# State-space layer: six PSUM banks in the ring, state outputs of two tiles in four array quarters, a reordered end of the gated unit

## The chip, the cores and the metric

The kernel runs on one core of one Trainium2 chip. The metric is the device time of one execution in microseconds (us). A core has TensorE (PE: matmuls, and transposes as matmuls against an identity), VectorE (DVE), ScalarE (ACT), GpSimd (POOL) and SyncE (SP, which here issues most of the DMAs), and sixteen DMA engines that carry what the queues hold. PSUM, into which PE writes, has eight banks of 2 KB in each of 128 partitions.

## The reference, cut to what matters

Two layers on 512 tokens of width 1024. Layer 0 mixes tokens by a diagonal complex state space (64 groups of 16 channels, 64 states each), followed by a gelu and a gated linear unit; layer 1 is attention. A dense feed-forward net follows layer 0, eight routed experts follow layer 1. The change lies in the mixer of layer 0:

```python
bu_re = jnp.einsum('bsgc,gpc->sbgp', ug, bb_re)
bu_im = jnp.einsum('bsgc,gpc->sbgp', ug, bb_im)
...
_, _, s_re, s_im = lax.associative_scan(_s5_combine, (a_re, a_im, bu_re, bu_im), axis=0)
y = (jnp.einsum('sbgp,gcp->bsgc', s_re, c_re.astype(f32))
     - jnp.einsum('sbgp,gcp->bsgc', s_im, c_im.astype(f32)))
y = y.reshape(bsz, seq, D_MODEL) + d_skip.astype(f32) * uf
act = jax.nn.gelu(y).astype(u.dtype)
val, gate = jnp.split(act @ w_glu, 2, axis=-1)
return val * jax.nn.sigmoid(gate)
...
x = _layer_norm(ALPHA * x + mix, ln_g[layer, 0], ln_b[layer, 0])
```

## The kernel before, in words

**The scan in blocks.** The 512 tokens are 64 blocks (j) of 8 steps (t). Inside a block the mixer is a matrix (Toeplitz blocks `s_T`, made from `s_K` by `s5_k`); between blocks a state `s_S` is carried by a scan on DVE over numbers that are turned to a rotating frame before it and back after it (`turn`, L1899: three DVE passes, L1905, L1906 and L1909, through the scratch tile `s5_ctv`). Complex products of coefficients go through `cmul` (L1798), in steps of at most 512 elements of each part, with the same scratch tile when DVE does them. All of it is done for two halves of the groups: half 0 feeds output pairs `dp` 0 and 1, half 1 pairs 2 and 3.

**The outputs.** `s5_y(dp)` (L2003) makes two output tiles i of [64 blocks, in two halves of 64 partitions for the parity of the group; 4 groups pairs q x 128 columns], each in one PSUM bank. For each q there are two matmuls of `s_T` (L2017: 128 rows, 64 columns of the array) and four of the state (L2021: 64 rows and 64 columns, real and imaginary part), in the order T T S S S S for each of the four q. ACT takes the gelu (L2023), and the result is also written to DRAM (`YD`, used only by a fallback path). `s5_act(dp)` (from L2031) transposes it (L2044), 16 transposes to a pair, and ACT and DVE split it in a high and a low half-precision part `xt` (L2047, L2048).

**The gated unit.** `w_glu` has 1024 x 2048 numbers. It is taken in four quarters of columns (256 of value, 256 of gate), and each quarter in two chunks of 1 MB, 8 chunks in all. A chunk is loaded by eight DMAs of [128 partitions, 256 columns] (`Stream.load`, L85), converted to two half-precision parts by ACT and DVE (`Stream.convert`, L102 and L103), and used by 48 matmuls with `mm3` (L275 to L277: three products for each pair of parts). All these DMAs are issued by SyncE in the program's order, as are X (L2127), the gain and bias of the norm (`gb`, L197) and the feed-forward weights behind them; chunk 0 comes early in the scan, chunk 1 behind the transfers that spread `s_K` (L2000). The unit's rows are ordered as the transposes leave them: in the weight's row index (k g r c) a tile has the eight values of g and the sixteen of c on its partitions.

**Where the two meet.** `glu_quarter` runs the first two quarters in four steps kp and calls `before(kp)` at each, for the first quarter this function of `run` (L2051):

```python
            def before(kp):
                if kp == 2:
                    self.s5_y(2)
                    self.s5_y(3)
                    self.s5_act(2)
                    self.s5_act(3)
                if kp == 3:
                    st.convert(3)
```

**The end of the unit.** `glu_last` (L307) does the last quarter token tile by token tile, in an order written out by hand in `GLU_ORDER` (L54): M is a tile's 24 matmuls, E its sigmoid and sum, s a step of its layer norm, T the transposes of the normalised tile (L261, L264, L265) for the feed-forward net, c a conversion of that net's weights, a and b the net's first blocks on the first and the second 256 tokens. PSUM banks are handed out by `bank()` from a ring of `nps`: 5 during the scan, 8 from the gated unit on; the other banks of the scan belong to the pool `pt` (the scratch tile and the coefficients `s5_pwp`).

Of the kernel before, what the change touches and what calls it, by code (L numbers as in the profile page):

```python
# [15 lines left out]
D = 1024  # L16
# [4 lines left out]
L = 8  # L21
# [29 lines left out]

GLU_FAST = (2, 3)
MLA_ORDER = "O0 R0 s0 s0 O1 R1 s1 s0 s1 O2 R2 s2 s1 s2 T0 O3 R3 s3 s2 s3 p0 T1 s3 g0 a0 T2 a1 A0 T3 a2 A1 r0 a3 q0 A2 r1 v0 q1 v1 t0 A3 r2 v2 t1 q2 r3 k0 v3 t2 q3 t3"
GLU_ORDER = "M0 c2 E0 s0 M1 M2 E1 s1 s0 s1 s0 s1 T0 E2 s2 s2 T1 M3 E3 s2 s3 s3 s3 a0 T2 T3 a1 b0 c4 c3 b1"  # L54
RSQRT = 519526879.0


# [66 lines left out]
class Kernel:  # L124
# [154 lines left out]

    def glu_chunks(self):  # L280

        w = self.A["s5_w_glu"][0].rearrange("(k g r c) (v n) -> k r g c v n", k=4, r=2, c=GC, v=2)
        return [[(w[kp, r, :, :, v, q * 256:(q + 1) * 256], o + v * 256, o + (v + 1) * 256, None)
                 for kp in (k2, k2 + 1) for r in range(2) for v in range(2) for o in ((kp - k2) * 1024 + r * 512,)]
                for q in range(4) for k2 in (0, 2)]

    def glu_mms(self, acc, tt, kp, w):

# [1082 lines left out]
    def general(self, flag):  # L1371
# [6 lines left out]
        with tc.If(reg > 0):  # L1378
# [77 lines left out]
                    V.tensor_copy(xt[:, 2 * dp:2 * dp + 2].rearrange("p r (j t) -> p r t j", t=L)[:, :, t0:t0 + 4],  # L1456
                                  b.rearrange("p (t r j) -> p r t j", t=4, r=2))
            nc.sync.dma_start(X, A["x"][0].rearrange("(t p) d -> p t d", p=128))
            wg = A["s5_w_glu"][0].rearrange("(k g r c) (v n) -> k r g c v n", k=4, r=2, c=GC, v=2)
            for c in (slice(0, 512), slice(512, 1024)):  # L1460
                b = [[bank() for _ in range(TT)] for _ in range(2)]
                for k in range(KD):
                    for v in range(2):
                        w = weights(wg[k // 2, k % 2, :, :, v, c])
                        for tt in range(TT):
                            mm(b[v][tt], xt[:, k, tok(tt)], w, start=k == 0, stop=k == KD - 1)
                for tt in range(TT):
# [198 lines left out]
    def s5_params(self):  # L1666
# [73 lines left out]
        for i in range(3):  # L1740
# [4 lines left out]
                V.tensor_sub(P[:, i, 0], t[:, 0], t[:, 1])  # L1745
                V.scalar_tensor_tensor(P[:, i, 2], re, 2.0, im, op0=OP.mult, op1=OP.mult)
            V.tensor_scalar(P[:, i, 1::2], P[:, i, 2, None, :].to_broadcast([128, 2, 32]), -1.0, None, op0=OP.mult)
        self.pwp = self.pt.tile([128, 3, 4, 32], F, name="s5_pwp")
        nc.scalar.activation(self.pwp, P, AF.Copy)
        self.bb = self.r3.tile([128, 2, 32, GC], F, name="s5_bb")  # L1750
        self.cmul(V, self.bb, self.b, f, 0, 32)
# [46 lines left out]
    def cmul(self, eng, dst, x, cf, g0, g1, conj=False, one=None):  # L1798


        n = x.shape[3]
        step = min(g1 - g0, 512 // n)
        cr = cf[:, 0, None, :, None]
        ci = cf[:, 2:4] if conj else cf[:, 1:3]
        nm = "s5_ctv" if eng is self.nc.vector else "s5_ctp"
        for g in range(g0, g1, step):
            s = slice(g, g + step)
            sh = [128, 2, step, n]
            if eng is self.nc.vector:
                t = self.pt.tile([128, 2, 512], F, name=nm, tag=nm, bufs=1)[:, :, :step * n]  # L1810
            else:
                t = self.r3.tile([128, 2, 512], F, name=nm, tag=nm, bufs=1)[:, :, :step * n]
            t = t.rearrange("p a (g n) -> p a g n", n=n)
            xs = x[:, :, s]
            eng.tensor_mul(t, self.swap(xs), ci[:, :, s, None].to_broadcast(sh))
            if n >= 64 and eng is self.nc.vector:
                for i in range(step):
                    eng.scalar_tensor_tensor(dst[:, :, g + i], x[:, :, g + i], one[:, 0, g + i:g + i + 1], t[:, :, i],
                                             op0=OP.mult, op1=OP.add)
                continue  # L1820
            eng.tensor_mul(dst[:, :, s], xs, cr[:, :, s].to_broadcast(sh))
            eng.tensor_add(dst[:, :, s], dst[:, :, s], t)
# [76 lines left out]
    def turn(self, dst, x, E, back):  # L1899
        V = self.nc.vector  # L1900
        sh = list(x.shape)
        t = self.pt.tile([128, 2, 512], F, name="s5_ctv", tag="s5_ctv", bufs=1).rearrange(
            "p a (i n) -> p (a i n)", n=4 * NJ)[:, :8 * NJ]
        t = t.rearrange("p (a g n) -> p a g n", a=2, g=4)[:, :, :, :sh[3]]
        V.tensor_mul(t, self.swap(x), E[:, 1, None].to_broadcast(sh))  # L1905
        V.tensor_mul(dst, x, E[:, 0, None].to_broadcast(sh))  # L1906
        for part in range(2):
            op = V.tensor_add if back == (part == 0) else V.tensor_sub
            op(dst[:, part], dst[:, part], t[:, part])  # L1909
# [92 lines left out]

    def s5_y(self, dp):  # L2003

        nc = self.nc
        mm = nc.tensor.matmul
        y = self.r1.tile([128, L, 2, 4, GC], F, name="s5_y", tag="s5_y", bufs=2)
        T = self.T[dp // 2]
        halves = [slice(par * 64, par * 64 + 64) for par in range(2)]
        for i in range(2):  # L2010
            dt = 2 * dp + i
            p = self.bank()
            for q in range(4):
                pr = dt * 4 + q
                c = slice(q * 128, (q + 1) * 128)
                for par, rows in enumerate(halves):
                    mm(p[rows, c], self.U[:, 2 * pr + par], T[:, (q % 2 * 2 + par) * 8 + q // 2 * 4 + dt % 4], start=True, stop=False,  # L2017
                       tile_position=(0, par * 64))
                for part in range(2):
                    for par, rows in enumerate(halves):  # L2020
                        mm(p[rows, c], self.S[rows, part, pr, 0:NJ], self.O[rows, part, pr], start=False,  # L2021
                           stop=part == 1, tile_position=(par * 64, par * 64))
            nc.scalar.activation(y[:, :, i].rearrange("j t q c -> j q t c"),  # L2023
                                 p.rearrange("j (q t c) -> j q t c", q=4, t=L), AF.Gelu_apprx_tanh)
        self.ydt[dp] = y
        nc.gpsimd.dma_start(self.YD[dp * 128:(dp + 1) * 128], y.rearrange("p t i q c -> p (t i q c)"))
# [24 lines left out]
    def run(self):  # L2051
# [6 lines left out]

        self.YD = dram.tile([SEQ, D], F, name="YD")
        if phases != "moe":  # L2060
            self.ps = self.pool("psS", None, space=bass.MemoryType.PSUM)
            self.nps = 5
            self.pt = self.pool("psT", None, space=bass.MemoryType.PSUM)
        else:
            self.ps = self.pool("psA", None, space=bass.MemoryType.PSUM)
        self.wp = self.pool("w", "right")
# [1 line left out]
        if phases != "moe":  # L2068
# [47 lines left out]
            self.bz = None  # L2116
            self.s5_scan(1, E[1])
            E = self.dec = None
            self.pt.release()
            self.ps.release()  # L2120
            self.nps = 8
            self.ps = self.pool("psA", None, space=bass.MemoryType.PSUM)
            st.load(2)
# [8 lines left out]
            def before(kp):  # L2132
                if kp == 2:
                    self.s5_y(2)
                    self.s5_y(3)
                    self.s5_act(2)
                    self.s5_act(3)
                if kp == 3:
                    st.convert(3)

            self.glu_quarter(0, st, before)
# [102 lines left out]
```

## Time and profile before

| | us |
|---|---|
| median of three runs | 1849.55 (1846.19 to 1849.65) |
| the profiled execution | 1850.73 |
| its span in the trace | 1849.0 |
| PE busy | 1721.1, 93% of the span |
| DVE busy | 1399.1, 76% |
| ACT busy | 1001.2, 54% |
| last scan matmul to first of the gated unit | 117.45 to 125.17 |
| first matmul of the last quarter (M0) | 207.73 |
| first matmul of the feed-forward net (a0) | 237.67 |

The profiled execution takes 1.73 us more than its span, which lies around it. PE is the engine that is busiest and also the one that the end of the program waits for most; the stretch that the change touches ends at a0, after 13% of the span. Times below are from the start of the span. A timeline row gives the start, the length, the line and the tiles of one or more like instructions, and in brackets how long the engine stood idle before them and what released it. The length of a matmul in a row contains its way through the array; matmuls follow each other faster than that, so a rate is read from the starts of successive rows.

### The profile page before, as it was taken

How to read it: one execution, taken by the hardware profiler on the slowest of the kernel's cores; microseconds unless marked ns; L12 is line 12 of the kernel's file. 1: busy time of each engine (PE TensorE's matmuls, PEld its weight loads, DVE VectorE, ACT ScalarE, POOL GpSimd, SP SyncE). 2: the span in 40 equal slices, each digit the busy share in tenths (PEclk: the TensorE clock that was granted, in tenths of full speed). 3: DMA queues.
4: the chain of work that ended last, by engine and by line, in shares of the span. 5: the costliest groups of instructions: out<-in, count | busy, mean ns of one | idle time of the engine just before them, and what ended most of it. 6: DMA issues, size and time to landing. Idle time of an engine off the chain costs nothing.

```text
span 1849.0 us, 45063 instructions
## 1 busy us (share of the span) xinstructions
PE 1721.1 (93%) x19531; PEld 1360.6 (74%) x19531; DVE 1399.1 (76%) x2040; ACT 1001.2 (54%) x1100; POOL 223.4 (12%) x232
## 2 busy tenths in 40 slices
PE   5689899999999898789999999999999999999984
PEld 4455464444446564589999999999999899999863
DVE  9863653333246784589999898999999799999987
ACT  4223432323142673277676666767667676766771
POOL 6910100000000101100000121210000100000035
PEclk9889999999999999789999999999999999999997
DMA  4236423332352000299999999999999999999991
GB/s 81 52 110 212 118 69 109 96 103 80 136 151 88 1 24 24 105 380 376 359 328 347 343 340 331 325 365 350 362 351 351 286 377 378 362 368 365 353 365 60
DMA packets 359393, 433.79 MB, mean 235 GB/s; under 512 B 30520, under 2 KB 321424, under 8 KB 359184
## 3 DMA queue, kind: packets, MB, share of 16 engines
q1 hardware_dynamic: 346832, 417.55, 67.0%
q0 software_dynamic: 4064, 12.72, 2.4%
q8 instruction: 155, 2.54, 0.6%
q10 hardware_dynamic: 8288, 0.54, 0.4%
q14 instruction: 54, 0.44, 0.1%
HBM read 416.81 MB, written 11.34 MB: 232 GB/s over the span
## 4 chain that ended last, share of the span: by engine, by line
PE 77%; DVE 12%; ACT 3%; DMA 3%; issue 3%; POOL 1%; POOLq 0%; DVEq 0%; ACTq 0%; SPq 0%
PE gu L275 10%; PE gu L277 10%; PE gu L276 10%; PE ps L276 7%; PE ps L277 7%; PE ps L275 7%; PE y L275 5%; PE y L277 5%; PE y L276 5%; DVE wi L1110 2%; PE gu L1058 2%; DMA mraw<-in_moe_w_in_dram 2%; PE glu L277 1%; PE glu L275 1%; PE glu L276 1%
## 5 line engine op out<-in xcount | busy, mean ns | idle before, releaser
L277 PE MATMUL gu<-xe,wi 128*128 128x132 f16 (+7 forms) x3584 | 660.3, 225 | 17.8 <-DVE wi L1110 17.7
L275 PE MATMUL gu<-xe,wi 128*128 128x132 f16 (+7 forms) x3584 | 660.5, 225 | 6.1 <-ACT yr L1195 4.1
L276 PE MATMUL gu<-xe,wi 128*128 128x132 f16 (+7 forms) x3584 | 660.3, 225 | 0.0
L1110 DVE SCALAR_TENSOR_TENSOR wi<-mraw,wi 128x2048 f16<-128x2048 f32 x224 | 512.0, 2286 | 9.0 <-ACT wi L1104 9.0
L1104 ACT ACTIVATE wi<-mraw 128x2048 f16<-128x2048 f32 x224 | 420.5, 1904 | 26.5 <-DMA mraw<-in_moe_w_in_dram 25.6
L277 PEld LDWEIGHTS <-wi 128*128 128x128 f16 x3584 | 352.7, 98 | 19.4 <-DVE wi L1110 19.4
L276 PEld LDWEIGHTS <-wi 128*128 128x128 f16 x3584 | 354.1, 99 | 9.2 <-issue 4.5
L275 PEld LDWEIGHTS <-wi 128*128 128x128 f16 x3584 | 353.2, 99 | 5.8 <-ACT wi L1104 2.1
L1110 DVE SCALAR_TENSOR_TENSOR wol<-mraw,woh 128x2048 f16<-128x2048 f32 x112 | 255.8, 2284 | 0.3 <-ACT woh L1104 0.3
L1104 ACT ACTIVATE woh<-mraw 128x2048 f16<-128x2048 f32 x112 | 213.3, 1904 | 7.8 <-DMA mraw<-in_moe_w_out_dram 7.8
L277 PE MATMUL y<-hh,wol 128*128 128x132 f16 (+4 forms) x1120 | 215.9, 227 | 0.0
L275 PE MATMUL y<-hh,woh 128*128 128x132 f16 (+4 forms) x1120 | 215.9, 227 | 0.0
L276 PE MATMUL y<-hl,woh 128*128 128x132 f16 (+4 forms) x1120 | 215.9, 227 | 0.0
L1127 ACT ACTIVATE hs<-gu 128x168 f32<-128x168 f32 (+5 forms) x224 | 63.8, 285 | 273.5 <-PE gu L277 273.1
L103 DVE SCALAR_TENSOR_TENSOR wf<-raw,wf 128x2048 f16<-128x2048 f32 x34 | 77.9, 2292 | 95.7 <-ACT wf L102 81.1
L1162 POOL DMA_INDIRECT XD<-yr,at x12 | 26.4, 2204 | 810.0 <-ACT yr L1195 444.3
L275 PE MATMUL ps<-xt,wf 128*128 128x512 f16 x320 | 121.3, 379 | 0.0
L276 PE MATMUL ps<-xt,wf 128*128 128x512 f16 x320 | 121.3, 379 | 0.0
L277 PE MATMUL ps<-xt,wf 128*128 128x512 f16 x320 | 121.3, 379 | 0.0
L1128 DVE SCALAR_TENSOR_TENSOR hf<-gu,hs 128x168 f32<-128x168 f32 (+5 forms) x224 | 66.7, 298 | 60.0 <-ACT hs L1127 59.3
L275 PEld LDWEIGHTS <-woh 128*128 128x128 f16 x1120 | 109.6, 98 | 0.0
L276 PEld LDWEIGHTS <-woh 128*128 128x128 f16 x1120 | 109.6, 98 | 0.1
(460 smaller groups left out, 2792.2 us busy)
## 6 DMA issues: line engine op xcount, KB each, us to landing
mraw<-in_moe_w_in_dram SPq DMA_DIRECT2D x224, 1024.0 KB
mraw<-in_moe_w_out_dram SPq DMA_DIRECT2D x112, 1024.0 KB
raw<-in_ffn_w_in_dram SPq DMA_DIRECT2D x44, 512.0 KB
raw<-in_ffn_w_out_dram SPq DMA_DIRECT2D x11, 1024.0 KB
raw<-in_s_w_glu_dram SPq DMA_DIRECT2D x64, 128.0 KB
raw<-in_mla_o_w_dram SPq DMA_DIRECT2D x4, 1024.0 KB
XD<-X SPq DMA_DIRECT2D x5, 512.0 KB
xj<-in_x_dram SPq DMA_DIRECT2D x4, 512.0 KB
```

What stands on the lines that cost most here:

```text
L103: nc.vector.scalar_tensor_tensor(lo[:, c], raw[:, c], scale[j], hi[:, c], op0=OP.mult, op1=OP.subtract)
L275: mm(out, lh, rh, start=first, stop=False, **kw)
L276: mm(out, lh, rl, start=False, stop=False, **kw)
L277: mm(out, ll, rh, start=False, stop=last, **kw)
L1058: nc.tensor.matmul(p[:, (k - k0) * cap:(k - k0 + 1) * cap], x[:, tt, k * 128:(k + 1) * 128], sel[:, tt, :cap], start=tt == 0, stop=tt == T ...
L1104: nc.scalar.activation(hi, raw, AF.Copy, scale=WS)
L1110: self.nc.vector.scalar_tensor_tensor(lo, raw, WS, hi, op0=OP.mult, op1=OP.subtract)
L1127: nc.scalar.activation(sg, p[:, :cap], AF.Silu, scale=1.0 / (WS * XS))
L1128: nc.vector.scalar_tensor_tensor(h, p[:, cap:2 * cap], HS / (WS * XS), sg, op0=OP.mult, op1=OP.mult)
L1162: self.nc.gpsimd.indirect_dma_start(out=self.XD, out_offset=bass.IndirectOffsetOnAxis(ap=self.at[:n, j:j + 1], axis=0), in_=yr[:n], in_off ...
```

## The change

Five edits: (1) the ring of the scan has six banks instead of five, for which the scratch tile is halved and `cmul` on DVE takes steps of 256 elements instead of 512; (2) `s5_y` is split in `s5_yt`, the T matmuls of both tiles, and `s5_ys`, the state matmuls of both tiles side by side, where the second tile's two parities land in swapped halves of the partitions, so that four consecutive state matmuls use the four quarters of the array; (3) the swap permutes the rows that the gated unit's weights must have, and each of its weight DMAs becomes two of 64 partitions; (4) the T matmuls of y(3) go ahead of the transposes of y(2), and `s5_act(3)` moves to kp 3; (5) in `GLU_ORDER` M3 goes ahead of T0, and a1 ahead of T2. The diff, cut (a fallback path that isn't run here gets the same two DMAs):

```diff
-GLU_ORDER = "M0 c2 E0 s0 M1 M2 E1 s1 s0 s1 s0 s1 T0 E2 s2 s2 T1 M3 E3 s2 s3 s3 s3 a0 T2 T3 a1 b0 c4 c3 b1"
+GLU_ORDER = "M0 c2 E0 s0 M1 M2 E1 s1 s0 s1 s0 s1 M3 T0 E2 s2 s2 T1 E3 s2 s3 s3 s3 a0 a1 T2 T3 b0 c4 c3 b1"
...
-        w = self.A["s5_w_glu"][0].rearrange("(k g r c) (v n) -> k r g c v n", k=4, r=2, c=GC, v=2)
-        return [[(w[kp, r, :, :, v, q * 256:(q + 1) * 256], o + v * 256, o + (v + 1) * 256, None)
-                 for kp in (k2, k2 + 1) for r in range(2) for v in range(2) for o in ((kp - k2) * 1024 + r * 512,)]
+        return [[(src, o + v * 256, o + (v + 1) * 256, view)
+                 for kp in (k2, k2 + 1) for r in range(2) for v in range(2) for o in ((kp - k2) * 1024 + r * 512,)
+                 for src, view in self.glu_rows(kp, r, v * D + q * 256, 256)]
                 for q in range(4) for k2 in (0, 2)]
+
+    def glu_rows(self, kp, r, c, n):
+        w = self.A["s5_w_glu"][0]
+        row = 2 * D
+        return [(bass.AP(tensor=w.tensor, offset=w.offset + (kp * 16 + i * 8 + (r ^ i)) * GC * row + c,
+                         ap=[[2 * GC * row, 4], [row, GC], [1, n]]), lambda d, i=i: d[i * 64:i * 64 + 64]) for i in range(2)]
...
-        step = min(g1 - g0, 512 // n)
+        step = min(g1 - g0, (256 if eng is self.nc.vector else 512) // n)
...
-                t = self.pt.tile([128, 2, 512], F, name=nm, tag=nm, bufs=1)[:, :, :step * n]
+                t = self.pt.tile([128, 2, 256], F, name=nm, tag=nm, bufs=1)[:, :, :step * n]
...
+    def s5_yt(self, dp):
...
         for i in range(2):
             dt = 2 * dp + i
             p = self.bank()
             for q in range(4):
+                for par in range(2):
+                    o = (par ^ i) * 64
+                    mm(p[o:o + 64, q * 128:(q + 1) * 128], self.U[:, 2 * (dt * 4 + q) + par],
+                       T[:, (q % 2 * 2 + par) * 8 + q // 2 * 4 + dt % 4], start=q == 0, stop=False,
+                       tile_position=(0, o), skip_group_check=True)
...
+        for q in range(4):
+            for part in range(2):
+                for i, p in enumerate(ps):
+                    pr = (2 * dp + i) * 4 + q
+                    for par in range(2):
+                        rows = slice(par * 64, par * 64 + 64)
+                        o = (par ^ i) * 64
+                        mm(p[o:o + 64, q * 128:(q + 1) * 128], self.S[rows, part, pr, 0:NJ], self.O[rows, part, pr],
+                           start=False, stop=part == 1 and q == 3, tile_position=(par * 64, o), skip_group_check=True)
...
-            self.nps = 5
-            self.pt = self.pool("psT", None, space=bass.MemoryType.PSUM)
+            self.pp, self.pt, self.ps = (self.pool("ps" + n, None, space=bass.MemoryType.PSUM) for n in "ptS")
+            self.nps = 6
...
                 if kp == 2:
                     self.s5_y(2)
-                    self.s5_y(3)
+                    late = self.s5_yt(3)
                     self.s5_act(2)
+                    self.s5_ys(3, late)
+                if kp == 3:
                     self.s5_act(3)
-                if kp == 3:
                     st.convert(3)
```

How the instructions stand. First SyncE's queue from the second half's `s_K` transfers to the feed-forward weights, before (`raw` is a chunk of weights as loaded):

```order
L2000 DMA s_T<-s_K 32x8x32 x3
L85 DMA raw<-in_s_w_glu_dram 128x1x256 x8
L2127 DMA X<-in_x_dram 128x4x1024
L85 DMA raw<-in_s_w_glu_dram 128x1x256 x16
L197 DMA gb<-in_ln_g_dram 128x1024
L197 DMA gb<-in_ln_b_dram 128x1024
L85 DMA raw<-in_s_w_glu_dram 128x1x256 x32
L85 DMA raw<-in_ffn_w_in_dram 128x8x128 x44
```

and now:

```order
L2007 DMA s_T<-s_K 32x8x32 x3
L85 DMA raw<-in_s_w_glu_dram 64x1x256 x16
L2152 DMA X<-in_x_dram 128x4x1024
L85 DMA raw<-in_s_w_glu_dram 64x1x256 x32
L197 DMA gb<-in_ln_g_dram 128x1024
L197 DMA gb<-in_ln_b_dram 128x1024
L85 DMA raw<-in_s_w_glu_dram 64x1x256 x64
L85 DMA raw<-in_ffn_w_in_dram 128x8x128 x44
```

The order is the same; each weight DMA stands there as two of half the partitions.

Second, PE inside the first quarter, where y(2) and y(3) stand between the unit's steps kp 1 and kp 2. Before, the two rows of the start repeat sixteen times, and the transposes of both pairs follow together (`s_U` are the inputs, `s_O` the output coefficients, `s_y` the pair's result):

```order
L2017 MATMUL ps<-s_T,s_U 64x128 x2
L2021 MATMUL ps<-s_O,s_S 64x128 x4
L2017 MATMUL ps<-s_T,s_U 64x128 x2
L2021 MATMUL ps<-s_O,s_S 64x128 x4
...
L2044 MATMUL ps<-ident,s_y 128x128 x16
```

and now:

```order
L277 MATMUL glu<-wf,xt 128x512
L2026 MATMUL ps<-s_T,s_U 64x128 x16
L2044 MATMUL ps<-s_O,s_S 64x128 x32
L2026 MATMUL ps<-s_T,s_U 64x128 x16
L2068 MATMUL ps<-ident,s_y 128x128 x8
L2044 MATMUL ps<-s_O,s_S 64x128 x32
L275 LDWEIGHTS xt
L275 MATMUL glu<-wf,xt 128x512
```

PE changes between T and state matmuls four times instead of 32; the transposes of y(2) stand between T and state of y(3), and those of y(3) come after kp 2.

Third, PE at the end of the unit, where the transposes of the normalised tiles 0 and 1 (L261) stand. Before, M3 (matmuls into `glu`) follows them:

```order
L277 LDWEIGHTS xt
L277 MATMUL glu<-wp,xt 128x512
L261 MATMUL ps<-ident,X 128x128 x16
L275 LDWEIGHTS xt
L275 MATMUL glu<-wp,xt 128x512
```

and now it is ahead of them, and the feed-forward net's a0 (matmuls into `ps`) follows:

```order
L277 LDWEIGHTS xt
L277 MATMUL glu<-wp,xt 128x512
L261 MATMUL ps<-ident,X 128x128 x16
L275 LDWEIGHTS wp
L275 MATMUL ps<-xt,wp 128x256
```

The 24 matmuls of M3 have gone past T0 and T1.

## Rows read from the trace of the kernel before

**Rows 1.** Section 4 of the page, the chain that ended last, by engine
```profile
PE 77%; DVE 12%; ACT 3%; DMA 3%; issue 3%; POOL 1%; POOLq 0%; DVEq 0%; ACTq 0%; SPq 0%
```

**Rows 2.** Windows: stretch, length, busy of each engine, clock, DMA share, GB/s
```profile
157.00:211.00 54.00, 54.00 (x252) 24.49 (x251) 25.21 (x44) 19.02 (x21) 0.00 (x0) 1.00 0.70 201
162.00:178.00 16.00, 16.00 (x76) 7.28 (x75) 5.72 (x13) 4.48 (x6) 0.00 (x0) 1.00 0.55 184
186.00:204.00 18.00, 18.00 (x85) 8.16 (x84) 8.41 (x9) 6.13 (x5) 0.00 (x0) 1.00 1.02 271
1000.00:1400.00 400.00, 398.14 (x5716) 375.38 (x5715) 367.38 (x473) 272.44 (x247) 45.35 (x33) 1.00 1.02 347
```

**Rows 3.** Timeline of PE: start, length, line, operation, [idle before <- releaser]
```profile
106.75 0.44 PE L1988 MATMUL ps<-s_O,s_bz 128*64 128x128 f32 x4
...
125.17 0.58 PE L275 MATMUL glu<-wf,xt 128*128 128x512 f16 x1 [7.73 <-DVE s_S L1909]
...
130.67 0.43 PE L276 MATMUL glu<-wf,xt 128*128 128x512 f16 x1
```

**Rows 4.** Timeline of SyncE's queue (SPq), 118 to 180 us, and 161.57 to 178.45
```profile
126.54 5.20 SPq L85 DMA_DIRECT2D raw<-in_s_w_glu_dram  x8
...
132.35 17.49 SPq L85 DMA_DIRECT2D raw<-in_s_w_glu_dram  x16
...
161.58 16.86 SPq L85 DMA_DIRECT2D raw<-in_s_w_glu_dram  x24
```

**Rows 5.** DMA issues in 118 to 215 us: transfer, queue, count, KB each, us
```profile
YD<-s_y POOLq DMA_DIRECT2D x2, 512.0 KB, 6.6
```

**Rows 6.** Timeline of ACT, 137 to 219 us
```profile
137.66 1.91 ACT L102 ACTIVATE wf<-raw 128x2048 f16<-128x2048 f32 x1 [19.56 <-DMA raw<-in_s_w_glu_dram]
...
208.21 3.70 ACT L102 ACTIVATE wp<-raw 128x2048 f16<-128x2048 f32 x2
...
218.29 0.38 ACT L347 ACTIVATE glu_s<-glu 128x256 f32<-128x256 f32 x1 [1.19 <-PE glu L277]
```

**Rows 7.** Timeline of DVE, 55 to 237 us
```profile
55.05 0.69 DVE L1905 TENSOR_TENSOR s_ctv<-ps,s_E 128x504 f32<-128x504 f32 x1 [4.18 <-PE ps L1893]
...
79.49 0.74 DVE L1909 TENSOR_TENSOR s_S<-s_S,s_ctv 128x252 f32<-128x252 f32 x2
...
87.49 1.23 DVE L1815 TENSOR_TENSOR s_ctv<-s_O,s_pwp 128x1024 f32<-128x1024 f32 x1
...
98.20 0.69 DVE L1905 TENSOR_TENSOR s_ctv<-ps,s_E 128x504 f32<-128x504 f32 x1
...
210.15 4.49 DVE L103 SCALAR_TENSOR_TENSOR wp<-raw,wp 128x2048 f16<-128x2048 f32 x2 [0.90 <-ACT wp L102]
...
235.23 1.28 DVE L265 TENSOR_TENSOR xt<-ps,xt 128x512 f16<-128x512 f32 x2
```

**Rows 8.** Timeline of PE at the end of the gated unit
```profile
210.32 0.38 PE L275 MATMUL glu<-wp,xt 128*128 128x512 f16 x1
...
227.80 1.94 PE L261 MATMUL ps<-ident,X 128*128 128x128 f32 x8 [4.36 <-DVE X L249]
...
237.67 0.27 PE L275 MATMUL ps<-xt,wp 128*128 128x256 f16 x1
...
245.35 1.09 PE L261 MATMUL ps<-ident,X 128*128 128x128 f32 x8 [1.40 <-DVE X L219]
```

**Rows 9.** Timeline of PE in y(0), y(1), and in the block products after it
```profile
83.37 0.44 PE L2017 MATMUL ps<-s_T,s_U 128*64 128x128 f32 x4
83.74 0.65 PE L2021 MATMUL ps<-s_O,s_S 64*64 64x128 f32 x8
84.32 0.44 PE L2017 MATMUL ps<-s_T,s_U 128*64 128x128 f32 x4
...
98.61 0.69 PE L1893 MATMUL ps<-s_U,s_at 128*64 128x64 f32 x16
99.23 0.66 PE L1876 MATMUL ps<-ident,s_A 128*128 128x128 f32 x4
```

More of the change, by code (lines that the diff above doesn't have):

```diff
@@ L1458, in general @@
             nc.sync.dma_start(X, A["x"][0].rearrange("(t p) d -> p t d", p=128))
-            wg = A["s5_w_glu"][0].rearrange("(k g r c) (v n) -> k r g c v n", k=4, r=2, c=GC, v=2)
             for c in (slice(0, 512), slice(512, 1024)):
@@ L1463, in general @@
                     for v in range(2):
-                        w = weights(wg[k // 2, k % 2, :, :, v, c])
+                        w = p.tile([128, 512], F, name="gw0", tag="gw0", bufs=2)
+                        for src, view in self.glu_rows(k // 2, k % 2, v * D + c.start, 512):
+                            nc.sync.dma_start(view(w), src)
                         for tt in range(TT):
@@ L1747, in s5_params @@
             V.tensor_scalar(P[:, i, 1::2], P[:, i, 2, None, :].to_broadcast([128, 2, 32]), -1.0, None, op0=OP.mult)
-        self.pwp = self.pt.tile([128, 3, 4, 32], F, name="s5_pwp")
+        self.pwp = self.pp.tile([128, 3, 4, 32], F, name="s5_pwp")
         nc.scalar.activation(self.pwp, P, AF.Copy)
@@ L1901, in turn @@
         sh = list(x.shape)
-        t = self.pt.tile([128, 2, 512], F, name="s5_ctv", tag="s5_ctv", bufs=1).rearrange(
-            "p a (i n) -> p (a i n)", n=4 * NJ)[:, :8 * NJ]
+        t = self.pt.tile([128, 2, 256], F, name="s5_ctv", tag="s5_ctv", bufs=1).rearrange("p a n -> p (a n)")
         t = t.rearrange("p (a g n) -> p a g n", a=2, g=4)[:, :, :, :sh[3]]
@@ L2003, in s5_y @@
     def s5_y(self, dp):
-        nc = self.nc
-        mm = nc.tensor.matmul
-        y = self.r1.tile([128, L, 2, 4, GC], F, name="s5_y", tag="s5_y", bufs=2)
+        self.s5_ys(dp, self.s5_yt(dp))
+    def s5_yt(self, dp):
+        mm = self.nc.tensor.matmul
         T = self.T[dp // 2]
-        halves = [slice(par * 64, par * 64 + 64) for par in range(2)]
+        ps = []
         for i in range(2):
@@ L2013, in s5_y, with s5_ys @@
             for q in range(4):
[L2014 to L2022, printed above, removed]
+                for par in range(2):
[3 more added lines that the diff above has]
+                       tile_position=(0, o), skip_group_check=True)
+            ps.append(p)
+        return ps
+    def s5_ys(self, dp, ps):
+        nc = self.nc
+        mm = nc.tensor.matmul
+        y = self.r1.tile([128, L, 2, 4, GC], F, name="s5_y", tag="s5_y", bufs=2)
+        for q in range(4):
[7 more added lines that the diff above has]
+                           start=False, stop=part == 1 and q == 3, tile_position=(par * 64, o), skip_group_check=True)
+        for i, p in enumerate(ps):
             nc.scalar.activation(y[:, :, i].rearrange("j t q c -> j q t c"),
@@ L2060, in run @@
         if phases != "moe":
-            self.ps = self.pool("psS", None, space=bass.MemoryType.PSUM)
-            self.nps = 5
-            self.pt = self.pool("psT", None, space=bass.MemoryType.PSUM)
+            self.pp, self.pt, self.ps = (self.pool("ps" + n, None, space=bass.MemoryType.PSUM) for n in "ptS")
+            self.nps = 6
         else:
@@ L2118, in run @@
             E = self.dec = None
-            self.pt.release()
-            self.ps.release()
+            self.pwp = None
+            for p in (self.ps, self.pt, self.pp):
+                p.release()
             self.nps = 8
```

## The prediction

> **What bounds the kernel now.** The page first: TensorE (PE) makes 77% of the chain that ended last [rows 1]. The change touches only the state-space layer and the gated unit behind it, the first 250 us, so next I read, stage by stage, how busy PE is there, then the order of PE, DVE and ACT and what each wait ended on. From 157 to 211 us PE has 54.00 busy of 54.00 [rows 2]: in the unit every microsecond of PE is paid for. Ahead of the unit it isn't: PE stands 7.73 us for the last unrotation on DVE [rows 3]. Last I looked at what feeds the unit, since its weights arrive while it runs. In 162 to 178 us nothing but these weights moves: the DMA engines are busy 0.55 of the time at 184 GB/s. When the feed-forward weights move (sources of 128 rows side by side), the same queue has a share of 1.02 at 271 GB/s, and with the experts' weights 347 GB/s [rows 2]. SyncE issued 24 of the unit's transfers, 128 KB each, in 16.86 us, 0.7025 us each, against 0.65 (8 in 5.20) when nothing was ahead of them; and 16 issues right behind X's 2 MB took 17.49 us, 1.09 each [rows 4]. So SyncE was held back by transfers with half the engines idle: those of the unit use about half of the sixteen. That is the reading on which my forecast hangs.
>
> **The change, part by part.** The sum is made against the profiled execution, 1850.73 us, 1.18 above the median of the three runs; 1.2 comes off at the end.
>
> *1. Weight transfers.* One transfer of 128 rows, in 8 blocks of 16, becomes two of 64 rows, in 4 blocks of 16: 112 instead of 56 for chunks 1 to 7. A source of 8 blocks has half the engines busy, one of 128 has all [rows 2]: as if a block went to an engine as a whole. Then 4 blocks have a quarter of them, a half-size transfer lasts as long as a whole one did, 0.7025 us, and a chunk of 1 MB takes 16 x 0.7025 = 11.24 us instead of 5.62. PE eats a chunk in 10.4 us (48 matmuls of 0.2157), so weights turn from cover into bound. No row shows a source of 4 blocks; the bounds are 5.62 us a chunk (half the time each) and 11.24, and I take the upper, because the trace has the busy engines at their limit, not the bytes.
> The Trainium skill (DMA: Bandwidth & Descriptors, "Why a DMA increments its semaphore by 16 and not by 1") says that a transfer is spread over the largest number up to 16 that divides the slowest dimension of both sides, on the lowest-numbered engines: 8 before, 4 after. The trace's 0.55 agrees for 8; no run here shows 4 yet.
>
> *2. Start of the stream.* It waits for the second half's Toeplitz blocks (s5_k), whose transfers leave SyncE's queue at 126.54; s5_k starts on PE at 106.75, behind the gelu transposes [rows 3, 4]. After, those come earlier and s5_k waits instead for the third turn's read of a bank: turns start at 98.20 today [rows 7], 0.74 later by step 7, and run back to back at 2.13, the read ends 1.36 into its turn: 98.94 + 4.26 + 1.36 = 104.5. So 2.2 us earlier, 124.3 (bounds 124.3 and 126.5).
>
> *3. When chunk 7 lands.* 7 x 11.24 = 78.7. The same engines carry X (128x4x1024, 2.1 MB), ln_g and ln_b (128x1024 each, 1.05 MB together) and two writes of YD (1.05 MB) [rows 5]: 4.2 MB at 347 GB/s = 12.1. From the last issue to the landing: 5.9 us at most (chunk 1: 131.74 to ACT's start at 137.66, with X moving too), 0 at least; 2 taken, since SyncE is held back until near the end [rows 4, 6]. 124.3 + 78.7 + 12.1 + 2 = 217.1. ACT converts the chunk in 1.85 and DVE follows with 2.25 (half of 3.70 and of 4.49) [rows 6, 7]: 221.2. Before, PE took up that chunk at 210.32 [rows 8]: **+10.9**.
>
> *4. Clock.* PE is then idle for 7 to 8 us ahead of it (chunk 6 carries it to about 213). After the 7.73 us ahead of 125.17, 13 matmuls took 5.5 us instead of 2.8 [rows 3]: **+2.7**. M0 ends at 221.2 + 5.1 and M1 at 231.5.
>
> *5. The end of the unit.* Before, 9.5 us passed from the sigmoid of M1 (218.29) to T0 (227.80) [rows 6, 8]: tile 0 is normalised at 241.0. M2 and M3 now both run first, 2 x 5.18, to 241.9; M3 fills the 4.36 us in which PE stood before T0. T0 to the last eviction of T1 took 227.80 to 236.51, 8.7 us [rows 7, 8]; a0 needs only its first half, 0.6 sooner: 250.0. Before, a0 began at 237.67: **+12.4** so far, which is steps 3 and 4 less what the new order gives. PE stands about 5 us ahead of a0, for which the clock can cost 0 to 2.7; I take **+1.3**. With a1 ahead of T2 and T3 their wait of 1.40 us goes [rows 8], but b0 now stands right behind T3 and waits about as long for its eviction: 0. On ACT the conversion of two feed-forward chunks (c2) stands ahead of E0; they are queued behind chunk 7 and land about 6 us after it (2.1 MB at 347), converted near 228, still ahead of M1's end: 0, and 3 to 5 if they land late.
>
> *6. The state outputs.* y(2) and y(3) take 16 x 0.95 = 15.3 us on PE: 0.37 for four T records and 0.58 for eight S records, of which 0.16 a step is the change of array mode, as 16 records elsewhere take 0.62 [rows 9]. After: T 16 x 0.105 = 1.7, S between 1.7 (four quarters at once) and 3.4 (two), 2.5 taken, two changes of mode: 4.5 for a pair, 9.0 for both. Of the 6.3 saved, the gelu of y(2) and the transposes of y(3) show about 2 as waits: -4.3 (-2 to -5). It only brings PE sooner to chunks that aren't there: **0** in the sum. For y(0) and y(1) the saving lies under DVE: the S products wait for both unrotations of their pair (79.49 + 0.74 for the first) and DVE works on, alone, to 98.0 [rows 7].
>
> *7. cmul cut to 256 elements.* A 128x1024 step of 1.23 becomes two of 0.69 [rows 7]. Ahead of 98.0 one block of three such steps gains 0.44 and two of one such step 0.15 each: 0.74. In the preparation before 55.05 some 1.9 us are added, under DVE's 4.18 us of idle time there [rows 7]. The unit's start moves by 0 to +1, which PE then waits for anyway: 0.
>
> *8. Sixth bank.* It takes waits of PE for a bank away in the first 105 us, where DVE is the bound: 0 beyond step 2.
>
> Sum: 12.4 + 1.3 = **+13.7**, 1864.4 on the profiled execution, 1863 against the median. Behind a0 the same work follows in the same order, on a chain that is PE's, and passes the delay on whole.
>
> **The rivals.** *Faster: a transfer of half the rows takes half the time.* Then the weights are in time and step 6 is real: -4.3, and some -0.6 from the new order of the end: 1844.5 (1842.5 to 1848). For it: bytes and rows of each transfer are halved. Against: a share of 0.55 while SyncE is held back [rows 2, 4]. It decides at chunk 7's last issue: PE wants the chunk at 210.32 - 5, less 4.1 for converting and 5.9 to land, so by 195.3; that is 71 us from 124.3, less 1.5 for X and the two norm vectors, over 112 issues: 0.62 us each.
> *No change: SyncE's issuing is the bound, whatever the engines.* At 0.65 an issue the last is out at 124.3 + 72.8 + 1.5 = 198.6, landed at 204.5, converted at 208.6: -1.7; at 0.70, +4.2. 1848 to 1854. For it: 0.65 at an empty queue. Against: 1.09 behind X, which issuing alone doesn't explain.
> *Slower by more:* 3.9 of landing, a second clock drop of 2.7 between chunks 4 and 6, c2 late: up to +9 on mine, 1872.
> *The four quarters don't run at once:* S at 3.4. Under my forecast it changes nothing; under the first rival it costs 1.8.
> The Trainium skill (TensorEngine Tiling (Array Packing), "Key Properties") has four 64x64 tiles working independently and a drain when the mode changes; the 0.16 us of step 6 agree with the drain, and the trace has no row with four quarters.
>
> **How the numbers follow.** The runs shown lie 3.5 us apart, and 0.2%, 3.7 us, is about what a measurement of this kernel can tell from no change. Weights bound by a quarter of the engines, with its slower end: 0.77 (1855 to 1873). Half-time transfers: 0.12. Issue-bound: 0.08, mostly within 0.2%. The rest, 0.03, is spread. So faster 0.13, same 0.09, slower 0.78. Leaving out the faster rival (0.12) and the outer ends of the others, the range is 1849 to 1875.
>
> **What would show it.** Right: 112 weight issues at 0.7 us each that last to about 215 us; a DMA share near 0.3 and some 95 GB/s where only they move; ACT waiting for raw ahead of chunks 4 to 7; PE idle ahead of the second half of M0 and matmuls of 0.43 us behind it; y pairs of 4 to 5 us. Wrong: SyncE done with the weights by 200 us, a DMA share above 0.5 in a stretch with weights alone, or PE without a gap from the unit's start to M2.

## The result, and the profile after

The changed kernel takes 1868.49 us (median of four executions, 1867.44 to 1870.03) against 1849.1 us of the kernel before: +19.4 us, ratio 1.0107 with a 95% interval of 1.0094 to 1.0120. The forecast was 1863.0, range 1849 to 1875, slower with a chance of 0.78. Its mechanism is there in the profile; the size was 5.5 us short on the medians (19.4 for 13.9), and the places where it was short are named below.

The profiled execution of the changed kernel has a span of 1865.6 us, 16.6 more than the one shown of before. The page first, its chain by engine and by line, against [rows 1]:

```profile
span 1865.6 us, 45144 instructions
PE 71%; DVE 13%; DMA 8%; ACT 3%; issue 3%; SPq 1%; POOL 1%; POOLq 0%; ACTq 0%; DVEq 0%
PE gu L275 10%; PE gu L277 10%; PE gu L276 10%; PE ps L276 7%; PE ps L277 7%; PE ps L275 7%; PE y L275 5%; PE y L277 5%; PE y L276 5%; DMA raw<-in_s_w_glu_dram 4%; DMA mraw<-in_moe_w_in_dram 2%; DVE wi L1117 2%; PE gu L1065 2%; DVE wol L1117 1%; DMA mraw<-in_moe_w_out_dram 1%
```

DMA has gone from 3% to 8% of the chain and PE from 77% to 71%, and 4% are one transfer by name, the weights of the gated unit. Now the stretches that answer to [rows 2], columns as there:

```profile
157.00:211.00 54.00, 45.88 (x200) 19.89 (x201) 16.61 (x30) 12.13 (x14) 0.00 (x0) 0.97 0.32 106
180.00:196.00 16.00, 13.23 (x62) 5.87 (x60) 5.37 (x13) 3.23 (x5) 0.00 (x0) 1.00 0.27 94
```

PE, which had 54.00 of 54.00, has 45.88: 8.1 us of gaps inside the unit. Where only the weights move (180 to 196 us) the share is 0.27 at 94 GB/s, half of the 0.55 and 184 that stood in [rows 2]. SyncE's queue, against [rows 4]:

```profile
127.68 9.26 SPq L85 DMA_DIRECT2D raw<-in_s_w_glu_dram  x16
136.98 0.46 SPq L2152 DMA_DIRECT2D X<-in_x_dram  x1
137.99 29.97 SPq L85 DMA_DIRECT2D raw<-in_s_w_glu_dram  x32
169.64 47.87 SPq L85 DMA_DIRECT2D raw<-in_s_w_glu_dram  x64
```

The first 16 issues, into an empty queue, take 0.58 each. The last 64 take 0.748 each, held back by the transfers, while the DMA share says that three quarters of the engines' time is idle. The last of them ends at 217.51; in the kernel before it ended at 178.43. ACT's conversions and PE's first matmuls behind them, against [rows 6, 8]:

```profile
200.15 1.91 ACT L102 ACTIVATE wf<-raw 128x2048 f16<-128x2048 f32 x1 [5.89 <-DMA raw<-in_s_w_glu_dram]
211.59 1.91 ACT L102 ACTIVATE wp<-raw 128x2048 f16<-128x2048 f32 x1 [9.54 <-DMA raw<-in_s_w_glu_dram]
224.02 1.91 ACT L102 ACTIVATE wp<-raw 128x2048 f16<-128x2048 f32 x1 [10.52 <-DMA raw<-in_ffn_w_in_dram]
```

```profile
225.98 0.58 PE L275 MATMUL glu<-wp,xt 128*128 128x512 f16 x1 [7.57 <-ACT wp L102]
228.31 0.58 PE L276 MATMUL glu<-wp,xt 128*128 128x512 f16 x1 [1.74 <-DVE wp L103]
254.86 0.27 PE L275 MATMUL ps<-xt,wp 128*128 128x256 f16 x1 [2.97 <-ACT xt L264]
256.70 0.37 PE L276 MATMUL ps<-xt,wp 128*128 128x256 f16 x1 [1.57 <-DVE xt L265]
```

Chunks 5, 6 and 7 reach ACT about 12 us apart while PE needs 10.4 for one. (The releaser in a row is inferred; the last conversion is chunk 7's, whatever transfer its row names.) PE waits 7.57 and 1.74 us for chunk 7, starts the second half of M0 at 225.98 instead of 210.32, and a0 at 254.86 instead of 237.67.

**A mark for the front part.** Behind the gated unit all versions do the same work. In the dense feed-forward net PE runs in steps of 10.36 us, so I take the start of the tenth activation there as a mark: what stands at the mark is the whole effect of the front. Before, and after:

```profile
319.24 0.60 ACT L378 ACTIVATE ffn_s<-ps 128x512 f32<-128x512 f32 x1 [2.02 <-PE ps L277]
```

```profile
340.94 0.60 ACT L385 ACTIVATE ffn_s<-ps 128x512 f32<-128x512 f32 x1 [2.02 <-PE ps L277]
```

+21.7 us. From the mark to the end of the span the twelve profiled executions of this study took between 1524.7 and 1533.8 us, with no pattern by kernel that I can show. That spread is as large as the one between executions of one and the same kernel (the kernel before: 1844.87 to 1852.26 in the 54 executions beside the experiments), so a version's front is better judged at the mark than by one time. The mark has a spread of its own: the kernel before has it at 319.24 and 318.04, the changed kernel at 340.94 and 336.69.

### The profile page after: what moved, and what is told of

It is laid out like the page before. It is cut to its first block, busy times and chain, and to the rows that moved or that the text cites. A ratio compares the mean times of both kernels' runs of the same rounds, so it can differ in the third digit from the quotient of the medians.

```text
span 1865.6 us, 45144 instructions
## 1 busy us (share of the span) xinstructions
PE 1716.7 (92%) x19531; PEld 1358.5 (73%) x19531; DVE 1400.7 (75%) x2058; ACT 1000.6 (54%) x1100; POOL 220.9 (12%) x232
## 4 chain that ended last, share of the span: by engine, by line
PE 71%; DVE 13%; DMA 8%; ACT 3%; issue 3%; SPq 1%; POOL 1%; POOLq 0%; ACTq 0%; DVEq 0%
PE gu L275 10%; PE gu L277 10%; PE gu L276 10%; PE ps L276 7%; PE ps L277 7%; PE ps L275 7%; PE y L275 5%; PE y L277 5%; PE y L276 5%; DMA raw<-in_s_w_glu_dram 4%; DMA mraw<-in_moe_w_in_dram 2%; DVE wi L1117 2%; PE gu L1065 2%; DVE wol L1117 1%; DMA mraw<-in_moe_w_out_dram 1%
## 5 line engine op out<-in xcount | busy, mean ns | idle before, releaser
L277 PEld LDWEIGHTS <-wi 128*128 128x128 f16 x3584 | 351.6, 98 | 19.4 <-DVE wi L1117 19.4
L102 ACT ACTIVATE wf<-raw 128x2048 f16<-128x2048 f32 x34 | 64.5, 1899 | 101.4 <-DMA raw<-in_s_w_glu_dram 51.9
```

The costliest lines, as they stand in the source:

```text
L102: nc.scalar.activation(hi[:, c], raw[:, c], AF.Copy, scale=scale[j])
L277: mm(out, ll, rh, start=False, stop=last, **kw)
```

## The experiments

| kernel | edit | time, us (before beside it) | ratio, 95% | mark |
|---|---|---|---|---|
| before | | 1849.1 | | 319.24 |
| after | the change | 1868.49 (1849.10) | 1.0107 [1.0094, 1.0120] | 340.94 |
| e1_split | before + two 64-row DMAs | 1868.70 (1847.35) | 1.0110 [1.0096, 1.0125] | 338.11 |
| e2_spread | after, 16 blocks a DMA | 1853.21 (1847.35) | 1.0030 [1.0017, 1.0042] | 322.88 |
| e3_early | after, chunks 1, 2 early | 1848.64 (1847.35) | 1.0006 [0.9997, 1.0015] | 314.79 |
| e4_order | before + new end | 1848.43 (1847.35) | 1.0003 [0.9994, 1.0012] | 319.17 |
| e5_before_early | before, chunks 1, 2 early | 1849.46 (1847.81) | 1.0010 [1.0001, 1.0020] | 319.96 |
| e6_noswap | after without the swap | 1848.55 (1847.81) | 1.0006 [0.9996, 1.0015] | 316.32 |
| e7_both | e2 and e3 together | 1846.09 (1847.81) | 0.9989 [0.9980, 0.9998] | 313.39 |
| f1_after_again | after, second profile | 1865.82 (1848.08), one each | | 336.69 |
| f2_before_again | before, second profile | 1848.94 (1848.08), one each | | 318.04 |
| f3_early_one | after, chunk 1 early | 1856.26 (1848.08), one each | | 327.81 |

### The split alone

```diff
+        return [[(w[kp, r, i * 4:i * 4 + 4, :, v, q * 256:(q + 1) * 256], o + v * 256, o + (v + 1) * 256,
+                  lambda d, i=i: d[i * 64:i * 64 + 64])
...
+                 for i in range(2)]
```

> The kernel before, with one edit: each weight DMA of the gated unit becomes two of 64 rows in 4 blocks (no swap, nothing else). Theory (a transfer of 4 blocks has a quarter of the engines, the late weights cost the time): a stretch with weights alone shows a DMA share near 0.27 and some 94 GB/s, the 64 issues of chunks 4 to 7 take about 48 us, chunk 7 is converted near 226, and the time is 1864 to 1870 us. Rival (another edit of the change costs the time: the shorter cmul steps, the array quarters, the order of the end): the split alone stays within 4 us of the kernel before.

+21.3 us, as much as the whole change and a little over. A quarter of the array, the banks, the shorter steps and the new order are not in this kernel. Its stretch with weights alone, and the last 64 issues, read like those of the changed kernel, and PE waits for chunk 7 in the same way:

```profile
180.00:196.00 16.00, 13.15 (x61) 5.77 (x60) 5.37 (x13) 3.22 (x5) 0.00 (x0) 1.00 0.27 94
```

```profile
168.85 47.19 SPq L85 DMA_DIRECT2D raw<-in_s_w_glu_dram  x64
```

```profile
224.71 0.58 PE L275 MATMUL glu<-wp,xt 128*128 128x512 f16 x1 [7.78 <-ACT wp L102]
```

ACT converts chunk 7 from 222.75, 3 us sooner than I had it. So the split of the weight DMAs is enough for the loss by itself.

### The same DMAs with sixteen blocks

The gelu stores y with the channel ahead of the pair, which makes the channel the outermost dimension of the weights' rows: 16 blocks of 4 rows instead of 4 of 16. Number, size and rows of the DMAs stay.

```diff
-                         ap=[[2 * GC * row, 4], [row, GC], [1, n]]), lambda d, i=i: d[i * 64:i * 64 + 64]) for i in range(2)]
+                         ap=[[row, GC], [2 * GC * row, 4], [1, n]]), lambda d, i=i: d[i * 64:i * 64 + 64]) for i in range(2)]
...
-        y = self.r1.tile([128, L, 2, 4, GC], F, name="s5_y", tag="s5_y", bufs=2)
+        y = self.r1.tile([128, L, 2, GC, 4], F, name="s5_y", tag="s5_y", bufs=2)
```

> The changed kernel, its results y stored with the channel ahead of the pair, so that each 64-row weight DMA has 16 blocks of 4 rows instead of 4 blocks of 16; same number of DMAs, same bytes. Theory: all sixteen engines take part, issues are bound by SyncE at 0.58 to 0.60 us, chunk 7 lands near 200, the weights are never late, and the saving on the state outputs is seen: 1843 to 1848 us. Rival (the number of DMAs or their size costs the time, not the engines): 1860 us or more.

1853.21 us: 5.9 of some 20 us are left, the rival is out, but the weights were still late and my range was missed. The window with weights alone, the 32 issues behind X and the last 64, the time from an issue to its landing (last column), and PE at chunk 7:

```profile
170.00:190.00 20.00, 20.00 (x94) 9.07 (x93) 7.66 (x14) 5.36 (x6) 0.00 (x0) 1.00 0.34 100
```

```profile
135.87 25.58 SPq L85 DMA_DIRECT2D raw<-in_s_w_glu_dram  x32
162.73 41.67 SPq L85 DMA_DIRECT2D raw<-in_s_w_glu_dram  x64
```

```profile
raw<-in_s_w_glu_dram SPq DMA_DIRECT2D x32, 64.0 KB, 2.2
```

```profile
208.35 0.38 PE L275 MATMUL glu<-wp,xt 128*128 128x512 f16 x1 [3.92 <-ACT wp L102]
```

In that window nothing is queued any more: a transfer has landed 2.2 us after its issue. But an issue takes 0.651 us, not the 0.58 to 0.60 that I had taken from the empty queue of the 4-block form, so a chunk takes 10.4 us, exactly PE's pace, and a lateness from before is never made up: PE still waits 3.92 us for chunk 7. Much of that lateness arises behind X, where 32 issues take 25.58 us, 0.80 each. Here SyncE's issuing is the bound, the case that the prediction had as its second rival, at the pitch it named. The rival's sum had the last issue out at 198.6, with 1.5 us for X and the norm's two vectors; it came at 204.40. With this the three forms stand side by side: 4 blocks share 0.27, 8 blocks 0.55, and 16 blocks no longer the limit.

### The slow DMAs, but earlier

```diff
-            st.load(1)
+            st.load(3)
             self.s5_y(0)
```

> The changed kernel with its 4-block DMAs, but the loads of chunks 1 and 2 issued right behind chunk 0, when SyncE's queue is free until 119 us. Theory (what costs is only that the weights come late): five chunks instead of seven are left for the time after 127 us, chunk 7 lands near 195 to 200 us, and the time is 1843 to 1849 us, although the transfers are as slow as before. Rival (slow transfers disturb something else, or another edit costs the time): 1860 us or more.

SyncE's queue stood empty from 74 to 119 us; 32 more issues fit there, and the last 64 then end 25 us sooner, at the same slow pace. Its queue, ACT at chunk 7, and PE at T0:

```profile
64.78 32.68 SPq L85 DMA_DIRECT2D raw<-in_s_w_glu_dram  x48
143.14 49.22 SPq L85 DMA_DIRECT2D raw<-in_s_w_glu_dram  x64
```

```profile
198.55 1.91 ACT L102 ACTIVATE wp<-raw 128x2048 f16<-128x2048 f32 x1 [10.22 <-DMA raw<-in_ffn_w_in_dram]
```

```profile
223.05 1.06 PE L261 MATMUL ps<-ident,X 128*128 128x128 f32 x8 [1.28 <-DVE X L249]
```

Chunk 7 is converted from 198.55, PE's first gap behind the first quarter is the 1.28 us ahead of T0, and the loss is gone: 1848.64 us. What costs is the lateness of the weights, not the slowness of the transfers as such. With chunk 1 alone moved (f3_early_one) the effect is a part of it:

> The changed kernel with only chunk 1 of the weights issued early (e3_early did 1 and 2). Theory (weights late, a chunk of 4-block transfers is worth 11 to 12 us of the stream): chunk 7 is converted 9 to 12 us ahead of the changed kernel's 224 us, still 5 to 8 us late, so the feed-forward's tenth activation comes at 326 to 331 us, between the 314.8 of e3_early and the 340.9 of the changed kernel. Rival (all or nothing): within 2 us of either end.

```profile
210.67 1.91 ACT L102 ACTIVATE wp<-raw 128x2048 f16<-128x2048 f32 x1 [10.53 <-DMA raw<-in_ffn_w_in_dram]
```

210.67 instead of 224.02, 13.35 us ahead where 9 to 12 were expected (9.6 against the second profile of the changed kernel, which has 220.28), mark 327.81 as expected and one time of 1856.26: a dose, not all or nothing.

### All of the change but the swap

```diff
-                    o = (par ^ i) * 64
+                    o = par * 64
```

with the weights loaded as in the kernel before.

> The changed kernel without the swap: both tiles' parities land in the same halves, state matmuls two quarters of the array at a time, weights as one 128-row DMA of 8 blocks, all else (six banks, 256-element steps, T ahead of S, new order of the end) as changed. Theory: no weight is late, and 1844 to 1849 us; the state matmuls of a pair take 3.4 us instead of 1.9. Rival (another edit beside the weights costs some of the 19 us): 1853 us or more.

1848.55 us: taken together, the other edits cost none of the 19. State and T matmuls of a pair, without the swap and, in the first profile of the changed kernel, with it (each row is 32 T or 64 state records):

```profile
139.37 3.71 PE L2044 MATMUL ps<-s_O,s_S 64*64 64x128 f32 x64
143.01 1.97 PE L2026 MATMUL ps<-s_T,s_U 128*64 128x128 f32 x32
```

```profile
137.71 1.97 PE L2026 MATMUL ps<-s_T,s_U 128*64 128x128 f32 x32
139.61 1.98 PE L2044 MATMUL ps<-s_O,s_S 64*64 64x128 f32 x64
141.52 1.97 PE L2026 MATMUL ps<-s_T,s_U 128*64 128x128 f32 x32
146.01 1.91 PE L2068 MATMUL ps<-ident,s_y 128*128 128x128 f32 x8 [2.52 <-ACT s_y L2047]
147.85 2.77 PE L2044 MATMUL ps<-s_O,s_S 64*64 64x128 f32 x64
```

From start to start 3.64 us become 1.91: four quarters do run at once. It is the swap that buys this and the swap that asks for the split DMAs. In this profile the pairs y(2), y(3) take from 137.71 to 150.55, 12.8 us with 2.52 of a wait and 8 transposes in it, instead of 15.3. The wait is not usual: in the second profile of the changed kernel the stretch has none and takes 8.6 us (138.65 to 147.28), 7.6 without the transposes. Of the 7.6 us that PE saves there, e6_noswap, without the swap, has 4.2 (137.47 to 149.58, 12.1 with 1.0 of transposes): these come from the order of T and S, and the other 3.5 from the four quarters.

### The new end alone, and the early loads alone

e4_order is the kernel before with the new `GLU_ORDER` line, e5_before_early the kernel before with `st.load(3)`.

> The kernel before with the new order of the end of the gated unit alone (M3 ahead of T0, a1 ahead of T2). My sum gave it about -0.6 us at a0 and 0 behind it: 1847.5 to 1849.5 us. Rival: T0 and T1 finish later behind M3 and a0 then waits for their evictions on DVE, +1 to +3 us.

1848.43 us, mark 319.17: nothing. But not for the reason I gave. a0 starts 3.83 us sooner than before, and the same is lost again behind it:

```profile
233.84 0.37 PE L275 MATMUL ps<-xt,wp 128*128 128x256 f16 x1 [2.98 <-ACT xt L264]
235.68 0.37 PE L276 MATMUL ps<-xt,wp 128*128 128x256 f16 x1 [1.47 <-DVE xt L265]
247.96 1.91 PE L261 MATMUL ps<-ident,X 128*128 128x128 f32 x16
250.62 0.27 PE L275 MATMUL ps<-xt,wp 128*128 128x256 f16 x1 [0.75 <-ACT xt L264]
251.57 0.27 PE L276 MATMUL ps<-xt,wp 128*128 128x256 f16 x1 [0.68 <-DVE xt L265]
```

PE waits 2.98 and 1.47 us for T1's eviction, which M3 used to cover, runs a0's first matmuls at the low clock (0.42 us long instead of 0.27), and waits again behind T2 and T3. From a0 to the mark it is 85.3 us instead of 81.6. ACT's part of that eviction stands where it stood, in the kernel before and in e4_order:

```profile
233.50 1.06 ACT L264 ACTIVATE xt<-ps 128x512 f16<-128x512 f32 x2
```

```profile
233.21 1.06 ACT L264 ACTIVATE xt<-ps 128x512 f16<-128x512 f32 x2
```

The new order moves M3, and not what a0 waits for.

> The kernel before, with chunks 1 and 2 of the unit's weights issued right behind chunk 0, nothing else. Theory: in the kernel before no weight is late, so nothing is won or lost: within 1.5 us of the kernel before, and PE's first matmul of the feed-forward net at 237 to 238.5 us. Rival (the early transfers disturb the scan or what follows, which would hide part of what e3_early won): +2 us or more.

1849.46 us, ratio 1.0010 [1.0001, 1.0020], mark 319.96: nothing is won in the kernel before, as its weights are in time; the median lies 1.65 above, a little more than I allowed, and 0.7 of it stands at the mark (the unit starts at 126.29 instead of 125.17). The three kernels that load chunks 1 and 2 early start the unit at 126.18 to 126.29, the nine other profiles at 124.56 to 125.64: early transfers beside the scan seem to cost about 1 us there.

### Both cures

> The changed kernel with both cures: 16 blocks to a weight DMA and chunks 1 and 2 issued early. Theory: weights in time with more to spare than in either alone; the front part gains some 4 us on the kernel before (feed-forward's tenth activation near 315 us instead of 319), time 1843 to 1848 us. Rival (what e3_early won in the front is lost again behind it, for whatever reason): 1847 to 1850 us, no better than the kernel before.

1846.09 us, ratio 0.9989 [0.9980, 0.9998]: the only version below the kernel before, by 1.7 us, and 22 below the changed kernel. The front gains 5.85 us at the mark. That its median gains only 1.7, e6_noswap's +0.7 for 2.9 gained at the mark, and e3_early's +1.3 for 4.45, is **not settled**. Their profiled executions took 1847.52, 1845.28 and 1845.12 us, which is 0.3, 2.5 and 2.2 below the median of the kernel before beside them: even in the executions that have a trace, only part of what the mark shows is left at the end.

### Second profiles

> The changed kernel once more, for a second profile. In its first profile PE ran at the low clock from 105 to 112 us, and the weight stream began at 127.68 us, while the same code in e2_spread and e6_noswap ran at full clock there and began at 124.4 to 124.6. Theory (the start hangs on that clock): if this profile has full clock at 105 to 112 the stream begins near 124.5 and the feed-forward's tenth activation comes near 338 us instead of 341; with the low clock again, both stay. Rival (the start has another cause): the start doesn't go with the clock.

> The kernel before once more, for a second profile: how far do the stages of one kernel repeat? If the front part is as repeatable as its rows suggest, the feed-forward's tenth activation comes within 0.8 us of 319.2 us again, and what differs between executions (some 7 us between the fastest and the slowest shown) lies behind the dense feed-forward net.

The granted clock (the column after the five engines) and the start of the stream go together. Two windows of the changed kernel's first profile, then of its second, and of the second also the queue, ACT at chunk 7 and PE at a0:

```profile
100.00:105.00 5.00, 2.99 (x20) 2.30 (x20) 4.69 (x11) 2.17 (x4) 0.00 (x0) 0.67 0.00 0
105.00:112.00 7.00, 7.00 (x56) 5.86 (x54) 6.86 (x11) 0.00 (x0) 0.00 (x0) 0.50 0.00 0
```

```profile
100.00:105.00 5.00, 4.04 (x21) 3.47 (x22) 4.69 (x11) 2.39 (x4) 0.00 (x0) 0.66 0.00 0
105.00:112.00 7.00, 7.00 (x96) 5.90 (x98) 6.86 (x11) 0.60 (x1) 0.00 (x0) 1.00 0.01 2
```

```profile
124.31 9.26 SPq L85 DMA_DIRECT2D raw<-in_s_w_glu_dram  x16
166.17 47.84 SPq L85 DMA_DIRECT2D raw<-in_s_w_glu_dram  x64
```

```profile
220.28 1.91 ACT L102 ACTIVATE wp<-raw 128x2048 f16<-128x2048 f32 x1 [10.31 <-DMA raw<-in_ffn_w_in_dram]
```

```profile
251.11 0.37 PE L275 MATMUL ps<-xt,wp 128*128 128x256 f16 x1 [2.97 <-ACT xt L264]
```

In the first, PE had waited 2.12, 0.62 and 1.04 us for banks just ahead, and s_K was made at 0.50, the lower of the two levels (1.2 GHz); in the second, with waits of 2.71 and 0.76, at 1.00 (2.4 GHz). Both fell in the window before (0.67 and 0.66); the second was back at 1.00 when s_K began. The stream starts at 127.68 in the one and at 124.31 in the other, and the mark moves with it, 340.94 and 336.69. With the stream as the bound, 3.4 us of PE's clock 20 us ahead of the unit is 3.4 us at the conversion of chunk 7 (224.02 and 220.28 have 3.74 between them). The other profiles with the changed scan fit: s_K's transfers begin at 119.33 with a clock of 0.50 in that window, at 117.90 and 117.60 with 0.76 (e3_early, f3_early_one), and at 115.91 to 116.44 with 1.00 (the second profile, e2_spread, e6_noswap, e7_both). The kernel before repeats less well at the mark than I had said: 318.04, 1.2 us off, of which 0.6 are in the unit's start already. From the mark to the end its two profiles differ by 0.8 us, so that executions differ behind the dense feed-forward net, as the expectation had it, is not shown.

## Why the prediction was right, and where it was off

- **The mechanism** (step 1: half as many engines, the same time for half the bytes) was right in each of its signs: share 0.27 where "near 0.3" stood, 94 GB/s for 95, 0.748 us an issue for 0.7, ACT waiting for raw ahead of chunks 4 to 7, PE idle 7.6 us ahead of the second half of M0. e1_split shows that it is enough, e6_noswap that the other edits together cost nothing, e2_spread and e3_early that the loss goes with the lateness of the weights. The Trainium skill (DMA: Bandwidth & Descriptors, "Why a DMA increments its semaphore by 16 and not by 1") has the number of engines as the largest number up to 16 that divides the slowest dimension of both sides; the traces now agree for 4 (a share of 0.27) as for 8 (0.55), and with 16 blocks nothing is queued. They show shares, not which engines worked.
- **Step 2, the start of the stream**: 124.3 was said and 124.31 seen in the second profile, 127.68 in the first, outside the bounds of 124.3 and 126.5. The term lacked the clock: that it could be low while s_K is made, behind PE's new waits for banks. +3.4 in the first profile.
- **Step 3, the landing**: the sum for the issues came out (last one out at 215.1 by the sum, 214.0 and 217.5 seen), in part by luck: in the second profile the last 64 took 2.9 us more than at 0.7025 each, the first 16 took 2.0 less, and what stands between them, 32 issues, X and the norm's vectors, took 2.0 less than the sum gave it with YD. "2 taken" from the last issue to the landing was the mis-sized term: 6.3 and 6.5 us (214.01 to 220.28, 217.51 to 224.02, where ACT starts on the chunk), more than even the upper bound of 5.9. At 0.748 an issue these are 8 or 9 transfers still ahead of the last one, by estimate: a SyncE that is held back to the end has a queue in front of it, which is a reason against 2 and not for it.
- **Step 4, clock**: 13 matmuls at the lower level were forecast; there were 14 in the second profile (0.59 to 0.63 us each in their rows) and 8 in the first.
- **Step 5, the end**: in the second profile T0 came at 245.19 for 241.9, late by the landing (+3.2), and a0 at 251.11 for 250.0. The 8.1 us from T0 to a0 were read from the wrong eviction, DVE's (L265). What a0's first matmul waits for is ACT's (L264), which stood 5.7 us behind T0 in the kernel before as well (233.50 for 227.80): a0 followed T0 by 5.9 us. DVE's eviction holds a0's second matmul, 7.8 us behind T0, so what was won at a0 is lost again one matmul later. What I had put at +1.3 behind a0 was 4.0 (85.6 us from a0 to the mark instead of 81.6): the wait for T1's second part, the clock, and the waits behind T2 and T3. e4_order shows the same 3.8 in the kernel before; step 5 had counted the wait that goes ahead of T3 and the one that comes ahead of b0, and not a0's second wait of 1.48.
- **Step 6**: four quarters, 1.91 us for the state matmuls of a pair, where 2.5 was taken between 1.7 and 3.4. By the rows of e6_noswap and of the changed kernel a T record takes 0.0594 us (32 in 1.90) and a state record on two quarters 0.0569 (64 in 3.64); a step of 0.95 then has 0.26 for its two changes of mode, by estimate, where 0.16 was put. PE saves 7.6 us for the 6.3 of the sum, and the waits there are about 1 us (0.74 and 0.23 at kp 3) for the 2 taken. As said, it is worth nothing while weights are late. That e3_early, with weights in time, has 4.45 at the mark where -4.3 was the sum is in part luck: its unit starts 1.0 late, and takes 74.7 us to M0 instead of 82.6.
- **Steps 7 and 8**: the unit starts at 125.55 and 125.40 instead of 125.17, inside "0 to +1".
- **The rivals**: half-time transfers (0.12) did not come. That SyncE's issuing is the bound (0.08) is not true of the change, but of its cure: e2_spread, 1853.2 us, inside the 1848 to 1854 given for it, though at 0.65 an issue the rival's own sum was -1.7 us and not +5.9.
- **Behind a0** the delay was to pass on whole. At the mark it is 21.7 and 17.45 us, on the medians 19.4; the spread from the mark to the end is too wide to say more.

Put together for the second profile: 13.7 of the sum, +4.3 for the landing, -1.1 for the issues, -2.2 from T0 to a0, +2.7 behind a0 (4.0 for 1.3) make 17.4; its mark stands 336.69 - 319.24 = 17.45 above the one shown of before. In the first the mark stands 4.25 higher, of which 3.4 are the start of the stream.

## What to carry to other kernels

A DMA that is split in two is not two halves: here the halves had 4 blocks in their outermost dimension instead of 8, half the DMA share (0.27 for 0.55), and each held SyncE as long as the whole had (0.748 us for 0.70), and a stream that was hidden became the bound. Look at the DMA share of a stretch where only that stream moves and where the issuing queue is held back: a share of a half there says how little room is left. There are two cures, and each works without the other: put a dimension of 16 outermost (e2_spread, most of the loss), or use the time in which the queue is empty to issue the first chunks (e3_early, all of it).

## What was not expected of the hardware

The time of an issue on SyncE's queue depends on the form of the transfer: into a free queue 0.58 us for 64 rows in 4 blocks (16 in 9.26), 0.65 for 128 rows in 8 blocks (8 in 5.20), 0.651 for 64 rows in 16 blocks (64 in 41.67). For the same 64 rows, 16 blocks cost more issue time than 4; the cause is not shown. 112 such issues are 73 us, as long as PE's work on the seven chunks.

The same code lost its clock in two executions at about the same place (0.67 and 0.66 from 100 to 105 us), with waits of PE that come to 3.8 and 3.5 us in all. In one it was back for the next window (1.00 from 105 to 112 us), in the other it was not (0.50); why is not shown.
